# A hybrid decoder layer on one core: another task order and other priorities in the mixer, and a last post-norm by token block with a shorter root on VectorE

## The chip, the cores and the metric

One core of a Trainium2 chip runs the whole layer as one program. The metric is device time in microseconds (us), lower is better. The engines are TensorE (PE, with its weight loads shown apart as PEld), VectorE (DVE), ScalarE (ACT), GpSimd (POOL) and SyncE (SP), whose queue issues nearly all DMAs.

## The reference, cut to what matters

512 tokens, 1024 channels, fp32. One layer is a half-weighted SwiGLU feed-forward (FFN1), a token mixer with three branches, and a second half-weighted feed-forward (FFN2), each between two RMS norms.

```python
def rms_norm(x, gain):
    y = x * lax.rsqrt(jnp.mean(x * x, axis=-1, keepdims=True) + 1e-6)
    return y * gain
...
h = swiglu(rms_norm(x, ffn1_pre_norm), ffn1_w_gate, ffn1_w_up, ffn1_w_down)   # hidden width 2816
x = x + 0.5 * rms_norm(h, ffn1_post_norm)
u = rms_norm(x, mix_pre_norm)
# columns of u @ w_in feed: A native sparse attention (8 heads of 64), B gated DeltaNet (4 heads of 128,
# chunked, with a triangular solve), C cross-attention into 256 memory tokens (4 heads of 128)
merged = sum_b sigmoid(u @ w_branch_gate)[b] * (o_b @ w_branch_b)
x = x + rms_norm(merged @ w_out, mix_post_norm)
h = swiglu(rms_norm(x, ffn2_pre_norm), ffn2_w_gate, ffn2_w_up, ffn2_w_down)
x = x + 0.5 * rms_norm(h, ffn2_post_norm)          # the last post-norm, and the output
```

## The kernel before

Every large product is made of three fp32r matmuls (L117 to L119): each weight tile of 128x512 is loaded (`wraw`, DMA at L105), rounded on ScalarE (`whi`, L106), and the rest is taken by a subtraction (`wlo`, L109) on VectorE, or on GpSimd for every n-th load of a task when `pool_every` is n (0: never). A product of one output tile over 1024 channels is 24 matmuls of 128x512.

The layer runs in five parts: FFN1, its down projection (tasks of `order0`), the DeltaNet part of the mixer with the projections (`order`), attention and branch merge (`order2`), `w_out` with the mixer's post-norm (`order3`), then FFN2 with its own down projection and the last post-norm.

The order of the work is written out by hand in the table `PRM`. `tasks` calls one small function for each name of a list; the letter is the function, the digits its arguments. The framework gives every instruction a priority by its place in the program, `off` lifts a task by that many places, and at build time a planner with its own cost estimates fills one fixed queue for each engine from the instructions that it thinks ready, the first by priority ahead. On the chip each engine works through its queue in order and waits at the head. So a list entry does not fix a place, it moves a task's instructions in five queues, and a late input at the head holds back everything behind it on that engine.

Names of tasks that matter below. In `order`: `c` h s is a convolved projection for head h (24 matmuls, then VectorE and ScalarE), `h` h s its norm and transposes, `r`, `l`, `k` the decay rows and the small matrices of a head, `b` i the forward substitution for a pair of heads (30 dependent small VectorE operations, L719 and L721, with DMA round trips through DRAM, L712, L723, L726), `e` i its expansion (`Dm`, `DT`, L739), `d` i k a level of block inversion (L757 to L774, alternating PE and VectorE), `s` i n a chunk of the recurrence, `o` i the output norm (`dory`, `on`, L823, transposes `pot`), `z` a projection of 96 matmuls, `q` i a query projection, `x` w the input of the compression (16 VectorE additions `X`, L900), `f` and `p` the compression itself. In `order0`: `d` i a down projection half, `p` and `n` post-norm and norm, `t` the transposes, `k` h and `v` keys and values of the memory tokens (`mkv`, `pmv`). In `order2`: `K` the key stacks, `S`, `P`, `V`, `W` attention, `C` the compressed branch, `G`, `A`, `U` the cross-attention, `M` br j one merge tile. In `order3`: `s` the splits of the merged rows, `d` i h the product with `w_out` for token half i and column half h, `p`, `n`, `t` as above, `g` the load of the gain.

The last post-norm handles token blocks 0 and 1 together behind the first half of the FFN2 down projection, then block 2, then block 3, through `postnorm(last=True)` (L219): for each column half a square with a running sum on ScalarE (`junk`, L211), a product with the gain on VectorE (`pre`, L237), the sum of the two halves (`ssp`, L245), the root by 9 VectorE operations (`rsqrt`, L129 to L139), and the scaled addition to the residual. Blocks 0, 1 and 3 make that addition on VectorE (L260); block 2 (`spread=True`) scales on ScalarE (L257) and adds on GpSimd (L258). Each half is stored from SP's queue (L262). The last eight weight tiles of block 3 run behind those of block 2 on PE, so that block 2's post-norm has matmuls beside it and block 3's has none.

Of the kernel before, what the change touches and what calls it, by code (L numbers as in the profile page):

```python
# [10 lines left out]
F32 = mybir.dt.float32  # L11
F32R = mybir.dt.float32r
BF16 = mybir.dt.bfloat16
I32 = mybir.dt.int32
# [3 lines left out]
P = 128  # L18
# [15 lines left out]
PAD = 88  # L34


PRM = {'order': ['i', 'a', 'w', 'c01', 'h01', 'c00', 'c10', 'c02', 'r0', 'h00', 'h02', 'c12', 'k0', 'h10', 'c22', 'l0', 'c11', 'h11', 'h12', 'r1', 'z', 'k1', 'c21', 'l1', 'h22', 'b0', 'c20', 'h21', 'e0', 'r2', 'h20', 'c32', 'l2', 'c31', 'd00', 'h31', 'k2', 'r3', 'c30', 'd01', 'l3', 'b1', 'd02', 'x0', 's00', 'e1', 'd10', 'h32', 'x1', 'd11', 'h30', 's01', 's02', 's03', 'q0', 'p0', 'o0', 'k3', 'p1', 'q3', 'p2', 'p3', 'd12', 's10', 'p4', 'q1', 'p5', 's11', 'p6', 'p7', 's12', 'q2', 'f', 's13', 'o1'], 'dma': {'l': 'sync', 'b': 'sync', 'd': 'scalar', 'c': 'sync', 'r': 'sync'}, 'off': {'b0': 300, 'h31': 400, 'h00': 20, 'r1': 50, 'h32': 50, 'h11': 200, 'h12': 200, 'd10': 100, 'A01': 100, 'A10': 100, 'A11': 100, 'A20': 100, 'A31': 100, 'A21': 200, 'x0': 20, 'x1': 20, 'C2': 50, 'L': 200, 'S310': 400, 'S001': 20, 'S311': 400, 'A30': 100, 'r0': 400, 'd02': 20, 's11': 50, 'V20': 400, 'l3': 100, 'q1': 20, 'f': 400, 'l1': 20, 'h20': 100, 'h22': 100, 'r3': 50, 'P010': 100, 'y': 100, 'h02': 50, 'S101': 20, 'A00': 100, 'Q0': 50, 'Q1': 50, 'Q2': 50, 'Q3': 50, 'P110': 400, 'V31': 50, 'd01': 200, 'o0': 400, 'p0': 50, 'p1': 50, 'p2': 50, 'p4': 50, 'p5': 50, 'p6': 50, 'p7': 50, 'b1': 20, 'h01': 100, 'M15': 20, 'P201': 400, 'e0': 100, 'e1': 100, 'o1': 20, 'q0': 50, 'q2': 20, 'h21': 20, 'd11': 50, 'p3': 50}, 'ph': 'e', 'po': 'ss', 'xpd': (0, 1, 2), 'order2': ['K1', 'K0', 'B', 'M10', 'C3', 'Q0', 'C0', 'Q1', 'S000', 'S001', 'P001', 'C1', 'P000', 'S010', 'C2', 'S011', 'V00', 'P010', 'S100', 'P011', 'S110', 'Q2', 'V01', 'P100', 'S101', 'W0', 'P101', 'S111', 'Q3', 'M12', 'V10', 'P110', 'S200', 'P111', 'S210', 'V11', 'P200', 'M14', 'S201', 'M15', 'P201', 'S211', 'W1', 'V20', 'P210', 'M11', 'P211', 'V21', 'S301', 'S300', 'W2', 'P301', 'S311', 'P300', 'L', 'M13', 'S310', 'G0', 'V30', 'P310', 'G2', 'M16', 'P311', 'V31', 'W3', 'A00', 'M00', 'M17', 'A01', 'G1', 'U0', 'A10', 'M05', 'A11', 'G3', 'A30', 'A31', 'U1', 'U3', 'M03', 'A20', 'A21', 'U2', 'M07', 'M22', 'M02', 'M20', 'M24', 'M06', 'M27', 'M21', 'M01', 'M26', 'M23', 'M04', 'M25'], 'order0': ['d0', 'p0', 'n0', 't0', 'd1', 'k2', 'k0', 'p2', 'p3', 'k1', 'n1', 'v', 'k3', 't1'], 'order3': ['s2', 's3', 's7', 's6', 's1', 's5', 's0', 's4', 'd01', 'd00', 'g', 'p0', 'd10', 'n0', 't0', 'd11', 'p1', 'n1'], 't3': (('mm', 'r'), ('e', 's')), 'pool': {'W2': 2, 's13': 3, 'k0': 0, 'k1': 0, 'k2': 0, 'k3': 2, 'p3': 1, 'C0': 0, 'C1': 0, 'C2': 0, 'C3': 2, 'S310': 0, 'L': 3, 'd11': 3, 'p0': 1, 'p1': 1, 'p2': 1, 'p4': 2, 'p5': 1, 'p6': 1, 'p7': 1, 'S311': 0, 'h01': 0, 'h00': 0, 'h02': 0, 'h10': 0, 'h11': 0, 'h12': 0, 'h22': 0, 'h21': 0, 'h20': 0, 'h31': 0, 'h30': 3, 'h32': 0, 'i': 2, 'P011': 2, 'c21': 0, 'd01': 2, 'S000': 0, 'S001': 0, 'S010': 0, 'S011': 0, 'S100': 0, 'S101': 0, 'S110': 0, 'S111': 0, 'S200': 0, 'S201': 0, 'S210': 0, 'S211': 0, 'S300': 0, 'S301': 0, 'M24': 2, 'G2': 2, 'A01': 0, 'M10': 2, 'M15': 2, 'M12': 2, 'M14': 2, 'M13': 2, 'M17': 2, 'M11': 2, 'M16': 2, 'M23': 0, 'M27': 3, 'M01': 2, 'M00': 2, 'M03': 0, 'M07': 2, 'M06': 0, 'M22': 2, 'M04': 2, 'M20': 2, 'M26': 3, 'M02': 0, 'M21': 2, 'M25': 2, 'M05': 2, 'c11': 1, 'o1': 3, 'P000': 2, 'P001': 1, 'P010': 2, 'P100': 2, 'P101': 2, 'P110': 2, 'P111': 2, 'P200': 2, 'P201': 2, 'P210': 2, 'P211': 2, 'P301': 0, 'P300': 2, 'P310': 2, 'P311': 2, 'c12': 0, 'b1': 1, 'x0': 0, 'x1': 0, 'V21': 0, 'c30': 0, 'c01': 0, 'c02': 0, 'c00': 0, 'c10': 0, 'c22': 0, 'c20': 0, 'c31': 0, 'c32': 0, 's01': 3, 'A31': 0, 'd12': 0, 'y': 2, 'G0': 2, 'G1': 2, 'G3': 2, 'U3': 0, 'W3': 2, 'r1': 2, 's12': 3, 'U2': 0, 'Q0': 2, 'Q1': 2, 'Q2': 2, 'Q3': 1, 's00': 3, 's02': 2, 's03': 3, 's10': 3, 's11': 3, 'e1': 2, 'd00': 1, 'U0': 0, 'U1': 0, 'l2': 0}, 'pool3': {'d00': 3, 'd01': 3, 'd10': 3, 'd11': 3, 'p1': 2, 't1': 3, 't0': 3, 's5': 2, 's7': 2, 's1': 2, 's0': 2, 's3': 2, 's6': 2, 's2': 2, 's4': 2, 'q0': 1}, 'pool0': {}, 'off0': {'p3': 20, 'n1': 50, 't1': 100}, 'off3': {'s1': 20, 's5': 200, 'g': 200, 't0': 400}, 'tt': ('e', 's'), 'order_s': ['t00', 'w10', 'w00', 'y', 't01', 't02', 'w01', 't03', 'w11', 'R0', 'F000', 'x', 'F101', 'n', 'F200', 't10', 't11', 't12', 't13', 'c', 'F110', 'B', 'F211', 'F011'], 't0': ('e', 's'), 'rs': ((0, 0), (0, 0)), 'ra': (1, 1), 'warm': 8, 'pools': {'F000': 0, 'F101': 0, 'F200': 0, 'F011': 0, 'F110': 0, 'F211': 0, 'w10': 0, 'w11': 0, 't00': 0, 't01': 0, 't02': 0, 't03': 0, 't13': 0, 't10': 0, 't11': 0, 't12': 0, 'w00': 0, 'w01': 0}, 'ptc': 'vvs', 'cva': 'v', 'offs': {'t13': 100, 'R1': 400}, 'vnc': 's', 'sp3': 0, 'hsc': 'vv', 'sf2': 2, 'psc': 'vvvv', 'sp1': 0, 'vbs': 'v', 't1c': 'vs', 'sgv': 256}


class Body:  # L40
# [84 lines left out]
    def rsqrt(self, ss, n, scale, eps, name):  # L125
# [13 lines left out]
        v.scalar_tensor_tensor(y, z, 1.5 * c, y, op0=OP.add, op1=OP.mult)  # L139
        return y  # L140

    def norm(self, xs, tbs, spread=False, junk=()):

        nc = self.nc
        n = len(tbs)
        ss = self.sp.tile([P, n], F32, tag=f"ss{n}", name="ss")
        for i, b in enumerate(tbs):
            jk = junk[i] if junk else self.tp.tile([P, D], BF16, tag="tmpa", bufs=2, name="junk")
            if spread:
                nc.vector.tensor_tensor_reduce(jk, xs[b], xs[b], 1.0, 0.0, op0=OP.mult, op1=OP.add, accum_out=ss[:, i : i + 1])  # L150
            else:
                nc.scalar.activation(jk, xs[b], AF.Square, accum_out=ss[:, i : i + 1])
        r = self.rsqrt(ss, n, 1.0 / D, EPS, "rn")
        for i, b in enumerate(tbs):
            nc.vector.tensor_scalar(xs[b][:, :512], xs[b][:, :512], r[:, i : i + 1], None, op0=OP.mult)
            nc.scalar.activation(xs[b][:, 512:], xs[b][:, 512:], AF.Copy, scale=r[:, i : i + 1])
# [62 lines left out]
            self.nc.vector.tensor_scalar(gb, gb, float(f), None, op0=OP.mult)  # L219
        return gb  # L220

    def postnorm(self, acc, x, gb, sc, tbs, store, tmp, pre=None, s2=None, last=False, spread=False, early=False):

        nc = self.nc
        n = len(tbs)
# [10 lines left out]
                    t = pre[h, i] = tmp()  # L236
                    nc.vector.tensor_tensor(t, acc[h][i], gb[:, h], op=OP.mult)  # L237

        if last or early:
            gain(0)  # L240
        self.sumsq(acc[1], s2, 1, n)
        if early:
            gain(1)
        ss = self.sp.tile([P, n], F32, tag="ssp", name="ssp")
        nc.vector.tensor_tensor(ss, s2[:, 0], s2[:, 1], op=OP.add)  # L245
        if last:
            gain(1)
        r = self.rsqrt(ss, n, sc * sc / D, EPS, "rp")
        if sc != 1.0:
            nc.vector.tensor_scalar(r, r, float(sc), None, op0=OP.mult)  # L250
# [2 lines left out]
        for i, b in enumerate(tbs):  # L253
            for h in range(2):
                c = slice(h * 512, h * 512 + 512)
                if spread:
                    nc.scalar.activation(pre[h, i], pre[h, i], AF.Copy, scale=r[:, i : i + 1])  # L257
                    nc.gpsimd.tensor_tensor(x[b][:, c], x[b][:, c], pre[h, i], op=OP.add)  # L258
                else:
                    nc.vector.scalar_tensor_tensor(x[b][:, c], pre[h, i], r[:, i : i + 1], x[b][:, c], op0=OP.mult, op1=OP.add)  # L260
                if last:
                    nc.sync.dma_start(store[b * P : (b + 1) * P, c], x[b][:, c])  # L262
            if not last:
                nc.sync.dma_start(store[b * P : (b + 1) * P], x[b])

    def ffn_tile(self, n, f, t, xh, xl, RB, H, banks=None, tags=("mm", "mm"), pre=None):

# [836 lines left out]
    def run(self):  # L1104
# [241 lines left out]
        with tc.tile_pool(name="f2", bufs=1) as fp, contextlib.ExitStack() as x1:  # L1346
# [33 lines left out]
            for tbs, acc in parts:  # L1380
                for h in range(2):
                    t0 = tbs[0] * P
                    step = (lambda k: self.hsplit(H, Hh, Hl, k, slice(t0, t0 + 256))) if h == 0 else None
                    self.down_half(Hh, Hl, "ffn2_d", FT, tbs, acc[h], h, lor if h and t0 else (), step, t0)
            self.post_gain("ffn2_post", 0.5, gb)
            pre = self.cp.tile([P, 4, 512], F32, tag="mth", name="pre")
            pre = iter([pre[:, i % 4] for i in range(8)])
            tmp = lambda: next(pre)
            (tbs, acc), (_, c) = parts
            self.postnorm(acc, x, gb, 1.0, tbs, self.out, tmp, last=True)  # L1390
            for i in range(2):
                self.postnorm([c[0][i : i + 1], c[1][i : i + 1]], x, gb, 1.0, (2 + i,), self.out, tmp, last=True, spread=i == 0)


def host_layout(i):
# [98 lines left out]
```

## Time and profile before

| what | value |
|---|---|
| median of three runs | 1378.45 us (1367.98, 1378.45, 1382.18) |
| the profiled execution | 1365.18 us, span 1363.4 us |
| TensorE busy | 1332.1 us, 98% of the span |
| VectorE, ScalarE, GpSimd busy | 897.0, 719.1, 146.1 us |
| mean granted clock of TensorE | 0.996 |

The span runs from the first to the last instruction. A matmul is shown busy for longer than the step to the next one, so a busy PE says that work is in flight, not that it runs at its peak.

### The profile page before, as it was taken

To read this page: it belongs to the slowest core of one execution; us is meant where nothing else is said; L and a number is where in the kernel's file an instruction comes from. 1 tells how busy PE (TensorE), PEld (TensorE's weight loads), DVE (VectorE), ACT (ScalarE), POOL (GpSimd) and SP (SyncE) were. 2 spreads that over 40 slices of the span, in tenths; PEclk is the share of its full clock that TensorE was granted. 3 is DMA by queue.
4 is the path that set the end of the run, shared out by engine and by line. 5 is a ranking of instruction groups with operands and counts; after the bars stand their busy time and mean duration, and the time that the engine had idled before them with its cause. 6 is when DMAs were issued, how large, how long until landed. Compare 5 with 4: busy or idle time off the path is not lost.

```text
span 1363.4 us, 21808 instructions
## 1 busy us (share of the span) xinstructions
PE 1332.1 (98%) x7839; PEld 1130.3 (83%) x7839; DVE 897.0 (66%) x1797; ACT 719.1 (53%) x1542; POOL 146.1 (11%) x132
## 2 busy tenths in 40 slices
PE   9999999999999999999999999999999999999997
PEld 8889999787887878677777777888788899998886
DVE  6897875777558576646876424223587778766765
ACT  7556664766555553216654334323585565646643
POOL 0020000000011312003110121333300000000000
PEclk9999999999999999999999999999999999999999
DMA  7643331676654332423121222532744433317673
GB/s 254 194 147 109 109 110 32 209 244 209 190 176 125 98 100 63 113 82 118 46 63 47 70 63 92 164 100 93 243 136 148 134 121 98 121 33 261 194 224 101
DMA packets 107453, 178.32 MB, mean 131 GB/s; under 512 B 18908, under 2 KB 28496, under 8 KB 107344
## 3 DMA queue, kind: packets, MB, share of 16 engines
q1 hardware_dynamic: 107056, 176.67, 41.8%
q8 instruction: 61, 1.00, 0.3%
q14 instruction: 48, 0.39, 0.1%
q10 hardware_dynamic: 288, 0.26, 0.1%
HBM read 166.84 MB, written 10.01 MB: 130 GB/s over the span
## 4 chain that ended last, share of the span: by engine, by line
PE 49%; DVE 3%; ACT 1%; issue 1%; DVEq 0%; ACTq 0%
PE pfm L119 5%; PE pfm L117 5%; PE pfm L118 5%; PE smm L406 5%; PE se L406 3%; PE po L1051 2%; PE ss L406 2%; PE ps L1019 2%; PE ppt L1039 1%; PE acc_mm L117 1%; PE acc_mm L118 1%; PE acc_mm L119 1%; PE acc_e L118 1%; PE acc_e L117 1%; PE acc_e L119 1%; PE acc_s L117 1%
## 5 line engine op out<-in xcount | busy, mean ns | idle before, releaser
L106 ACT CAST whi<-wraw 128x512 fp32r<-128x512 f32 (+1 forms) x314 | 189.8, 616 | 185.3 <-PE pfm L119 70.3
L109 DVE TENSOR_TENSOR wlo<-wraw,whi 128x512 fp32r<-128x512 f32 (+1 forms) x270 | 184.1, 690 | 143.6 <-ACT whi L106 139.6
L118 PE MATMUL pfm<-xth,wlo 128*128 128x512 f32 x384 | 154.9, 405 | 2.6 <-DVE wlo L109 2.6
L117 PE MATMUL pfm<-xth,whi 128*128 128x512 f32 x384 | 155.7, 406 | 1.1 <-DVE drz L134 0.7
L119 PE MATMUL pfm<-xtl,whi 128*128 128x512 f32 x384 | 154.0, 402 | 0.0
L118 PEld LDWEIGHTS pfm<-xth,wlo 128*128 128x128 f32 x384 | 72.3, 189 | 19.3 <-DVE wlo L109 3.2
L117 PEld LDWEIGHTS pfm<-xth,whi 128*128 128x128 f32 x384 | 72.4, 189 | 18.5 <-issue 3.9
L119 PEld LDWEIGHTS pfm<-xtl,whi 128*128 128x128 f32 x384 | 72.4, 189 | 15.4 <-issue 1.0
L109 POOL TENSOR_TENSOR wlo<-wraw,whi 128x512 fp32r<-128x512 f32 (+1 forms) x41 | 51.1, 1246 | 243.0 <-ACT whi L106 196.4
L106 ACT CAST ringh<-ringr 128x512 fp32r<-128x512 f32 x82 | 50.1, 620 | 42.4 <-DMA ringr<-in_ffn_d_dram 11.2
L406 PE MATMUL smm<-thi,fset 128*128 128x256 f32 x384 | 69.5, 279 | 0.0
L109 DVE TENSOR_TENSOR wlo<-ringr,ringh 128x512 fp32r<-128x512 f32 x75 | 51.4, 689 | 21.8 <-PE acc_e L119 8.7
L406 PEld LDWEIGHTS smm<-thi,fset 128*128 128x128 f32 x384 | 58.5, 188 | 0.2
L422 DVE TENSOR_TENSOR up<-smm,s 128x256 f32<-128x256 f32 x32 | 13.6, 424 | 67.2 <-ACT se L419 67.2
L406 PE MATMUL smm<-thi,fxtl 128*128 128x256 f32 x192 | 53.6, 279 | 0.6 <-DVE fxtl L388 0.6
L406 PE MATMUL smm<-thi,fxth 128*128 128x256 f32 x192 | 53.3, 278 | 0.0
L406 PE MATMUL se<-thi,fset 128*128 128x256 f32 x256 | 46.7, 280 | 0.0
L1022 ACT ACTIVATE Pm<-Pm,nm 128x128 f32<-128x128 f32 (+1 forms) x64 | 35.6, 557 | 11.9 <-DVE nm L1021 11.6
L258 POOL TENSOR_TENSOR xb<-xb,pre 128x512 f32<-128x512 f32 x2 | 2.5, 1277 | 356.7 <-ACT pre L257 356.7
L123 DVE TENSOR_TENSOR Hl<-H,Hh 128x256 fp32r<-128x256 f32 x88 | 35.0, 420 | 7.0 <-ACT Hh L122 5.5
L406 PEld LDWEIGHTS se<-thi,fset 128*128 128x128 f32 x256 | 39.1, 187 | 0.0
L379 DVE TENSOR_TENSOR fs<-fq 128x1024 f32<-128x1024 f32 x32 | 38.9, 1217 | 0.0
(550 smaller groups left out, 3979.3 us busy)
## 6 DMA issues: line engine op xcount, KB each, us to landing
wraw<-in_ffn_d_dram SPq DMA_DIRECT2D x94, 256.0 KB, 2.9
ringr<-in_ffn_d_dram SPq DMA_DIRECT2D x82, 256.0 KB, 2.9
fq<-in_ffn_g_dram SPq DMA_DIRECT2D x64, 256.0 KB, 2.9
fq<-in_ffn_u_dram SPq DMA_DIRECT2D x64, 256.0 KB, 2.7
wraw<-in_w_gate_dram SPq DMA_DIRECT2D x48, 256.0 KB, 2.8
wraw<-in_ffn_u_dram SPq DMA_DIRECT2D x34, 256.0 KB, 3.2
wraw<-in_ffn_g_dram SPq DMA_DIRECT2D x34, 256.0 KB, 3.5
woraw<-in_w_out_dram SPq DMA_DIRECT2D x32, 256.0 KB, 2.9
```

Source lines behind the costliest of these rows:

```text
L106: nc.scalar.copy(hi, raw)
L109: eng.tensor_tensor(lo, raw, hi.bitcast(F32), op=OP.subtract)
L117: t.matmul(out, lh, rh, start=first, stop=False)
L118: t.matmul(out, ll, rh, start=False, stop=False)
L119: t.matmul(out, lh, rl, start=False, stop=last)
L123: return self.nc.vector.tensor_tensor(lo, src, hi.bitcast(F32), op=OP.subtract)
L379: add = lambda *x: v.tensor_tensor(*x, op=OP.add)
L406: m = lambda x, y, **kw: te.matmul(out, x, y, skip_group_check=True, **kw)
L1019: te.matmul(s[:, : max(n, 256)], A[:, qb * P : qb * P + P], K[j][:, : max(n, 256)], start=j == 0, stop=j == 1)
L1022: nc.scalar.activation(pm, pm, AF.Exp, bias=nm[:, qb : qb + 1], scale=-1.0, accum_out=sm[:, qb : qb + 1])
L1039: te.transpose(pt[:, o : o + P], Pm[:, self.OFF[qb] + kb * P : self.OFF[qb] + kb * P + P], self.ident)
L1051: te.matmul(po[64 * g : 64 * g + 64, kb * P :], vt[:, kb, br * P + 64 * g : br * P + 64 * g + 64], pts[g][:, col[kb] : col[kb] + n], start ...
```

## The change

1. `order`, `order0`, `order2`, `order3` list the same tasks in another order, and some priorities (`off`, `off0`, `off3`, `offs`) and shares of GpSimd (`pool`, `pool3`) differ.
2. The last post-norm runs through a new function `ending`, one token block at a time, always on VectorE. The gain carries the constant `RK`, the root is `rsqrt1`: 7 operations, of which the first adds the two halves' sums of squares.

```diff
-'order': i a w c01 h01 c00 c10 c02 r0 h00 h02 c12 k0 h10 c22 l0 c11 h11 h12 r1 z k1 c21 l1 h22 b0 c20 h21 e0 r2 h20 c32 l2 c31 d00 h31 k2 r3 c30 d01 l3 b1 d02 x0 s00 e1 d10 h32 x1 d11 h30 s01 s02 s03 q0 p0 o0 k3 p1 q3 p2 p3 d12 s10 p4 q1 p5 s11 p6 p7 s12 q2 f s13 o1
+'order': i a w c01 h01 r0 c00 c10 c02 l0 h00 h02 c12 k0 h10 c22 c11 h12 h11 h22 r1 k1 l1 b0 c21 z h21 e0 c20 r2 h20 c32 l2 c31 d00 h31 k2 r3 d01 l3 b1 d02 x0 s00 e1 d10 c30 h32 x1 d11 h30 s01 s02 s03 q0 q3 p0 o0 p1 p2 p3 k3 d12 s10 p4 q1 p5 s11 p6 p7 s12 s13 o1 q2 f
-'order0': d0 p0 n0 t0 d1 k2 k0 p2 p3 k1 n1 v k3 t1
+'order0': d0 p0 n0 t0 d1 k2 k0 p2 p3 v k3 n1 k1 t1
-'order2': K1 K0 B M10 C3 Q0 C0 Q1 S000 S001 P001 C1 P000 S010 C2 ... P110 S200 P111 S210 V11 P200 ... W3 A00 M00 M17 A01 G1 U0 A10 M05 A11 G3 A30 A31 U1 U3 M03 A20 A21 U2 M07 M22 M02 M20 M24 M06 M27 M21 M01 M26 M23 M04 M25
+'order2': K1 K0 B M10 Q0 C0 Q1 S000 C3 S001 P001 P000 C1 S010 C2 ... P110 M12 S200 P111 V11 P200 S210 ... M17 V31 W3 A00 M00 A01 G1 U0 M05 A10 A11 G3 A30 U1 A31 U3 M03 M06 A20 A21 U2 M07 M22 M20 M02 M24 M27 M21 M23 M01 M04 M26 M25
-'order3': s2 s3 s7 s6 s1 s5 s0 s4 d01 d00 g p0 d10 n0 t0 d11 p1 n1
+'order3': s3 s7 s2 s6 s1 s5 s0 s4 d00 d01 d11 g p0 n0 t0 d10 p1 n1
 # priorities, old -> new (0: none)
 off:  b1 20->200  s00 0->200  s13 0->50  s11 50->100  c20 0->50  c11 0->20  k2 0->20  h00 20->0  p5 50->20  Q1 50->200  C2 50->0  P011 0->400  P010 100->50  M14 0->200  M03 0->20  A20 100->400  A21 200->20  U0 0->100
 off0: d0 0->200  k1 0->400  k2 0->400  t1 100->0
 off3: d10 0->200  p0 0->200
 offs: w10 0->200  t03 0->20
 # every n-th subtraction on GpSimd, old -> new (0: none); entries of tasks that load weights
 pool: K1 2->3  M10 2->1  M06 0->1  G3 2->0
 pool3: d11 3->0
```

```diff
+    RK = -0.5 * 0.375**3
+    def rsqrt1(self, s0, s1, scale, eps):
+        v = self.nc.vector
+        m, y, z = (self.sp.tile([P, 1], F32, tag=f"r1{s}", name=f"r1{s}") for s in "myz")
+        v.tensor_scalar(m, s1, float(scale), s0, op0=OP.mult, op1=OP.add)
+        v.tensor_scalar(y.bitcast(I32), m.bitcast(I32), -0.5, 1597463007.0, op0=OP.mult, op1=OP.add)
+        v.scalar_tensor_tensor(z, y, m, y, op0=OP.mult, op1=OP.mult)
+        v.scalar_tensor_tensor(z, z, -10.0 / 3, z, op0=OP.add, op1=OP.mult)
+        v.scalar_tensor_tensor(y, z, 5.0, y, op0=OP.add, op1=OP.mult)
+        v.scalar_tensor_tensor(z, y, m, y, op0=OP.mult, op1=OP.mult)
+        v.scalar_tensor_tensor(y, z, -3.0 / 0.375**2, y, op0=OP.add, op1=OP.mult)
+        return y
+    def ending(self, acc, x, gb, b, store, tmp):
+        nc = self.nc
+        s = self.sp.tile([P, 2], F32, tag="s21", name="s21")
+        pre = [tmp(), tmp()]
+        for h in range(2):
+            jk = self.tp.tile([P, 512], BF16, tag="tmpa", bufs=2, name="junk")
+            nc.scalar.activation(jk, acc[h], AF.Square, accum_out=s[:, h : h + 1])
+            nc.vector.tensor_tensor(pre[h], acc[h], gb[:, h], op=OP.mult)
+            if not h:
+                nc.vector.tensor_scalar(s[:, :1], s[:, :1], 1.0 / D, EPS, op0=OP.mult, op1=OP.add)
+        r = self.rsqrt1(s[:, :1], s[:, 1:], 1.0 / D, EPS)
+        for h in range(2):
+            c = slice(h * 512, h * 512 + 512)
+            nc.vector.scalar_tensor_tensor(x[b][:, c], pre[h], r, x[b][:, c], op0=OP.mult, op1=OP.add)
+            nc.sync.dma_start(store[b * P : (b + 1) * P, c], x[b][:, c])
...
-            self.post_gain("ffn2_post", 0.5, gb)
+            self.post_gain("ffn2_post", 0.5 * self.RK, gb)
...
-            (tbs, acc), (_, c) = parts
-            self.postnorm(acc, x, gb, 1.0, tbs, self.out, tmp, last=True)
-            for i in range(2):
-                self.postnorm([c[0][i : i + 1], c[1][i : i + 1]], x, gb, 1.0, (2 + i,), self.out, tmp, last=True, spread=i == 0)
+            for tbs, acc in parts:
+                for i, b in enumerate(tbs):
+                    self.ending([acc[0][i], acc[1][i]], x, gb, b, self.out, tmp)
```

`postnorm` loses its branches `last` and `spread`; what is left of it is what the other two post-norms ran before.

## Rows read from the trace of the kernel before

**Rows 1.** Windows by stage: length, busy PE, PEld, DVE, ACT, POOL, granted clock, DMA.

```profile
393.00:636.00 243.00, 233.80 (x1337) 188.65 (x1336) 149.42 (x404) 104.18 (x250) 43.02 (x49) 0.99 0.35 99
636.00:954.60 318.60, 316.91 (x1505) 242.10 (x1504) 157.46 (x418) 137.35 (x328) 73.48 (x55) 1.00 0.28 86
...
1233.40:1355.20 121.80, 121.34 (x531) 98.91 (x529) 83.94 (x162) 70.67 (x146) 1.10 (x1) 1.00 0.67 202
1355.20:1363.40 8.20, 0.00 (x0) 0.00 (x0) 3.99 (x13) 0.69 (x2) 1.42 (x2) 0.81 0.34 129
sum 1363.40, PE 1332.12 PEld 1130.30 DVE 897.04 ACT 719.09 POOL 146.13; mean PE 166.52 PEld 141.29 DVE 112.13 ACT 89.89 POOL 18.27
```

**Rows 2.** The same view, 50 us of merge tiles (128x512 matmuls alone).

```profile
850.00:900.00 50.00, 50.00 (x217) 40.55 (x216) 14.76 (x23) 16.07 (x28) 15.71 (x11) 1.00 0.48 151
```

**Rows 3.** Timeline of the end: start, duration, engine, line, operation, idle and its releaser.

```profile
1354.10 2.51 POOL L258 TENSOR_TENSOR xb<-xb,pre 128x512 f32<-128x512 f32 x2 [356.74 <-ACT pre L257]
...
1355.75 0.19 ACT L211 ACTIVATION_READ_ACCUMULATOR junk<-acc_s 128x1 f32 x1
1355.98 0.65 DVE L245 TENSOR_TENSOR ssp<-s 128x1 f32<-128x1 f32 x1 [2.71 <-ACT junk L211]
1356.56 0.68 DVE L237 TENSOR_TENSOR pre<-acc_s,gb 128x512 f32<-128x512 f32 x1
1357.16 0.14 DVE L129 TENSOR_SCALAR rpm<-ssp 128x1 f32<-128x1 f32 x1
...
1358.68 0.16 DVE L139 SCALAR_TENSOR_TENSOR rpy<-rpz,rpy 128x1 f32<-128x1 f32 x1
1358.87 1.42 DVE L260 SCALAR_TENSOR_TENSOR xb<-pre,rpy,xb 128x512 f32<-128x512 f32 x2
```

**Rows 4.** Timeline, the same operations for block 2.

```profile
1325.02 0.69 DVE L237 TENSOR_TENSOR pre<-acc_e,gb 128x512 f32<-128x512 f32 x1 [0.71 <-ACT junk L211]
...
1350.43 0.16 DVE L245 TENSOR_TENSOR ssp<-s 128x1 f32<-128x1 f32 x1 [5.05 <-ACT junk L211]
```

**Rows 5.** Waits of PE from 393 to 636 us: total, times, longest.

```profile
PE pfm L118 <- DVE wlo L109: 2.6, 1, 2.6
PE pt L761 <- DVE Dm L739: 1.7, 1, 1.7
PE ptk L655 <- DVE kn L648: 1.7, 1, 1.7
PE pot L824 <- DVE on L823: 1.2, 1, 1.2
```

**Rows 6.** Timeline of DVE around the expansion of the first pair.

```profile
519.90 2.15 DVE L739 TENSOR_TENSOR Dm<-Dc,msk 128x512 f32<-128x512 f32 x2 [1.98 <-DMA Dc<-dD]
```

**Rows 7.** Timeline of DVE before the longest wait.

```profile
544.49 2.68 DVE L900 TENSOR_TENSOR X<-pfm,pos 64x248 f32<-64x248 f32 x7 [0.95 <-PE pfm L119]
...
553.12 0.68 DVE L109 TENSOR_TENSOR wlo<-wraw,whi 128x512 fp32r<-128x512 f32 x1
```

**Rows 8.** Windows just behind the longest wait.

```profile
554.00:556.00 2.00, 2.00 (x8) 1.18 (x8) 1.93 (x8) 0.00 (x0) 0.00 (x0) 0.70 0.47 131
556.00:558.00 2.00, 2.00 (x6) 0.48 (x4) 1.73 (x9) 0.00 (x0) 0.00 (x0) 0.50 0.04 8
```

**Rows 9.** Waits of PE from 242 to 393 us.

```profile
PE pmv L117 <- ACT mkv L517: 1.4, 1, 1.4
```

**Rows 10.** Waits of PE from 954.6 to 1030 us.

```profile
PE ptr L166 <- DVE xa L155: 1.3, 1, 1.3
PE acc_s L117 <- ACT whi L106: 1.0, 1, 1.0
```

**Rows 11.** Timeline of ACT before the wait of `acc_s`.

```profile
987.06 1.06 ACT L152 ACTIVATE junk<-xa 128x1024 bf16<-128x1024 f32 x1 [2.91 <-DVE xa L260]
```

**Rows 12.** The page's costliest groups: GpSimd's subtractions.

```profile
L109 POOL TENSOR_TENSOR wlo<-wraw,whi 128x512 fp32r<-128x512 f32 (+1 forms) x41 | 51.1, 1246 | 243.0 <-ACT whi L106 196.4
```

**Rows 13.** Timeline of the first matmul's wait.

```profile
7.53 0.39 PE L117 MATMUL pg<-xth,whi 128*128 128x256 f32 x1 [1.57 <-ACT whi L106]
```

## The prediction before the run

> **What bounds the kernel now.** I read the busy shares of the page first, then the windows by stage, then PE's waits stage by stage, then the timeline around each wait. The reader is to see that PE is busy for 1332.1 of 1363.4 us [rows 1]: all idle time of PE together is 31.3 us, and no order of tasks can give more than that, beside what PE loses at a lower clock. The idle time is not spread evenly. The DeltaNet stage (393 to 636 us) has 243.0 - 233.8 = 9.2 us of it, attention and merge only 318.6 - 316.9 = 1.7 us, FFN2's down projection 0.5 us, and the end, where PE has nothing left, 8.2 us [rows 1]. So the long `order2` list, which the change rewrites most, works on a stage with next to nothing to win; `order` and the end are where the time can move.
>
> **The end.** It is one chain on VectorE. ScalarE's last sum of squares is there at 1355.75 + 0.19 = 1355.94, and the scaled addition begins at 1358.87: 2.93 us [rows 3]. In them stand the sum of the halves (0.62 until the next start), the gain product (0.60, from 1356.56 to 1357.16) and nine root operations (1.71, or 0.19 each). The sum of the halves takes 0.65 us, where the same operation took 0.16 for block 2 [rows 3, 4]; it ends at 1356.63, and GpSimd's additions for block 2 end at 1354.10 + 2.51 = 1356.61 [rows 3]. I read that as VectorE held up by GpSimd.
> After the change the chain is the gain product, if it still stands behind the square, and seven operations: 0.04 + 0.60 + 7 x 0.19 = 1.97 us. That removes 2.93 - 1.97 = 0.96 us: the held-up sum, which the first root operation takes in, and two root operations. The two additions (1.42 for both) and the stores stay. Would the gain product run beside the square, 0.60 more would go, 1.56 in all. I take 0.96, since in the rows the product of block 2 is idle until the square of the same accumulator has ended, though nothing of the square goes into it [rows 4]; the new code also writes the square first.
> The Trainium skill gives a reason why the two are kept apart: "PSUM — Partial Sum Buffer", section "PSUM bank collisions raise a hardware error", has it that two engines must not be on one bank and the same partitions at once, readers included. By that rule the gain of the end is the 0.96, without it the 1.56; the row agrees with the rule.
> What moves onto VectorE is block 2's addition, two operations of 0.7 us, in a stretch in which VectorE stood idle for 2.71 us before the last sum [rows 3]. I cost it at nothing; if that cover were gone it would be 1.4 us. The first two blocks now take two short roots for one longer one, 6 small operations or 1.1 us more, beside matmuls in a stage where PE idles 0.5 of 121.8 us and VectorE is busy for 83.9 [rows 1]: nothing, with 1.1 us as the bound. The stores keep their places on SP's queue behind the last weight loads; block 2's leave earlier.
>
> **The DeltaNet order.** Four waits make 7.2 of the stage's 9.2 us [rows 5].
> - `Dm`, 1.7 us: the expansion `e0` waits for the round trip of `b0` through DRAM (VectorE was idle for 1.98 us until `Dc` landed) [rows 6]. The new list puts `z`, 96 matmuls, between `b0` and `e0`; at 50.0/217 = 0.23 us each [rows 2] that is 22 us of work for PE while the trip runs. I expect this wait gone.
> - `wlo`, 2.6 us, the longest: a subtraction stands in VectorE's queue behind the 16 additions `X` (7 of them 2.68 us), a root and half of `b1`'s substitution, from 544.49 to 553.12 [rows 7]. Behind it PE runs at a granted clock of 0.70 and then 0.50, the lower of its two levels, for 4 us [rows 8]: 0.3 x 2 + 0.5 x 2 = 1.6 us of full-speed work lost on top. The new list moves the projection `c30` (24 matmuls, 5.5 us) to just before `h32 x1`, and lifts `b1`, so that its chain runs ahead of the additions. Both work on this wait; neither removes the additions. If gone, 4.2 us.
> - `on`, 1.2 us: the output norm `o1` was the last task, now `q2` (24 matmuls) and `f` are behind it. I expect it covered.
> - `kn`, 1.7 us, `h01` at the stage's start: `r0` moves to just behind it, which adds work to the same queues; I count nothing.
>
> **The other lists.** `order0`: `pmv` waits 1.4 us for ScalarE to clear a bank of the key product [rows 9]; `v` now stands ahead of `n1` and `k1`, `k1` and `k2` are lifted; 1.4 us if gone. Behind `v` on ScalarE's queue are then the squares of `n1`, and `t1` and the first task of `order` wait for those: the bound on the bad side is the same 1.4. `order3`: `acc_s` waits 1.0 us for a rounded weight, because ScalarE's queue has the norm's square at its head (idle 2.91 us until the residual is there) [rows 10, 11]. `d10` is now lifted by 200, so its roundings go ahead of such squares, and `d11` comes earlier; 1.0 us if gone. The 1.3 us of `ptr` [rows 10] belong to the chain of post-norm and norm itself, which keeps the same two products as cover; I count nothing. `order2`: its stage has 1.7 us of idle time in all; nothing, within 1.7 either way. `w10` lifted: PE's first wait on a rounded weight is 1.57 us [rows 13]; the weight comes earlier, the activations later by one transfer; nothing, within 0.6 either way, which is about one rounding.
> Shares of GpSimd: `M06` takes 3 subtractions and `M10` one or two more, `G3` and `d11` give up three or four, so there is at most one more, of 1.25 us [rows 12], in a stage in which PE waits for almost nothing. I count nothing; the bound is the 1.25. Against this part speaks the Trainium skill, "SBUF — State Buffer", section "Who interferes with whom": an operation of VectorE with two inputs from SBUF and one of GpSimd that reads SBUF block each other fully. The trace agrees with it at the one place costed above (0.65 for 0.16); by that rule the moved subtractions would hold up VectorE by up to their own 1.25 us each, and it gives no other sum as long as PE has its weights ahead.
>
> **The sum.** The waits with a reason to go are 1.7 + 4.2 + 1.2 + 1.4 + 1.0 = 9.5 us. But the planner filled the old queues by its own estimates and did not see these waits, or it would have filled them; the new queues come out of the same estimates and will have waits of the same kind elsewhere. I take half, 4.75, as the net, and 0.96 at the end: 1365.18 - 5.7 = 1359.5 us against the profiled execution. The three runs shown lie 2.8, 13.3 and 17.0 above that execution, 11.0 in the mean, by something that the profile does not show; so I forecast 1359.5 + 11 = 1370.5, say 1370, against the median of 1378.45. A measurement of this kernel, with runs 1% apart, can tell about 1% from no change; 1% is 13.8 us.
>
> **The rivals.**
> 1. All the named waits go and none comes: 0.96 + 9.5, so 1354.7, or 1365.7 for runs. For it: each of them has a task moved into it or a priority that bears on it. Against: the waits [rows 5] come from fixed queues, and 27 priorities changed at once. Chance 0.2.
> 2. The waits only move, and the end alone gains: 1364.2, or 1375. For it: the stage's idle time is of one kind, a VectorE that is late, and VectorE's work is the same. Chance 0.2.
> 3. Slower: `c30` is missing where it was. In the old list it stands between `r3` and `d01`, and its 24 matmuls are PE's only wide work beside the inversion levels `d01` and `d02`, which alternate PE and VectorE. If it covered them fully, 5.5 us become idle time, and a wait of that length brings the clock down as the 2.6 us did, 1.6 more. With the waits otherwise as in 2: 1365.18 - 0.96 + 7.1 = 1371.3, or 1382 for runs. It decides if PE's waits on `T`, `px` and `DT` behind `d01` add up to more than the 4.2 us of `wlo`. Against it: `l3`, `k2` and `r3` leave other work near. Chance 0.15, of which a third is beyond 1% slower.
>
> **How the numbers follow.** The forecast has 0.45. The range goes from rival 1 with the fastest of the run offsets, 1354.7 + 2.8 = 1357, to rival 3 with the median offset, 1371.3 + 13.3 = 1384; the costs bounded above (1.4, 1.7, 1.25, 0.6) lie inside. Faster by over 1% is below 1364.7: half of rival 1, a quarter of the forecast, a tenth of rival 2, 0.23 in all. Slower by over 1% is above 1392: 0.05. Within 1%: 0.72.
>
> **What would show it.** At the end: no separate sum of the halves, no GpSimd at all behind 1350 us, and about 2.0 us from the last square's end to the first addition. In PE's waits between 393 and 636 us: `pt` from `Dm` and `pot` from `on` missing, `wlo` shorter, and the granted clock without its dip, so that PE's idle time there falls from 9.2 to some 5 us. In `order3` no wait of `acc_e` or `acc_s` on `whi`. The prediction is wrong if the stage's idle time stays at 9 us or grows behind `d01`, if idle time appears in attention and merge, or if the runs scatter about another offset than those of before.

## The result and the profile after

| | before | after |
|---|---|---|
| median of ten runs | 1378.12 us (1365.75 to 1382.18) | 1360.55 us (1358.28 to 1363.56) |
| the profiled execution | 1365.18 us, span 1363.4 us | 1360.60 us, span 1358.8 us |
| TensorE, VectorE, ScalarE, GpSimd busy | 1332.1, 897.0, 719.1, 146.1 us | 1330.2, 899.9, 717.7, 142.3 us |

The ratio of the means is 0.9898 [0.9865, 0.9931]: 1% faster. The medians lie further apart, 17.6 us or 1.3%, because the runs of before are of two kinds. The prediction said 1370 us (1357 to 1384), with 1359.5 for a profiled execution and 11 us on top for the runs. The profiled execution came out at 1360.6; the 11 us did not come at all.

One thing must be known for every comparison below: the runs of the kernel before lie in two groups, whatever chip they ran on. Of the ten beside the result four are at 1365.75 to 1367.98 and six at 1377.80 to 1382.18. In the later comparisons, where each run's mean granted clock is listed, the lower group has .995 to .998 and the upper .983 to .988. The kernel after has one group, at .994 to .999. So the 17.6 us between the medians are 5.9 us between the lower groups (1366.46 to 1360.55) and 11.7 us that the upper group adds to the median of before. Both executions profiled here are of the lower kind, so their traces can explain the first part only.

Stage by stage, by the start of the first matmul of each stage in the two traces:

| stage | before, us | after, us | difference |
|---|---|---|---|
| up to the first matmul | 7.53 | 9.49 | +1.96 |
| FFN1 | 235.34 | 235.04 | -0.30 |
| `order0` | 153.75 | 152.65 | -1.10 |
| `order` (DeltaNet) | 239.23 | 236.92 | -2.31 |
| `order2` (attention, merge) | 318.81 | 319.11 | +0.30 |
| `order3`, FFN2's wide products | 279.40 | 276.87 | -2.53 |
| FFN2's down projection | 121.10 | 121.08 | -0.02 |
| last matmul to the end | 8.21 | 7.64 | -0.57 |

These are two single executions, and other traces tell which differences repeat. `order0` took 153.3 and 153.9 us in two further traces with the old lists (`e1`, `e2` below) and 151.6 and 152.0 in two with the new ones (`e3`, `e4`); `order3` with FFN2's wide products took 279.3 and 279.2 against 277.3 and 277.4. But `order` took 237.8 and 236.8 with the old list and 237.8 and 237.7 with the new one. The executions with the old list spread over 2.4 us (239.2 for before, and these two), so the 2.31 us of the table are within the scatter: between executions of the lower kind no gain of the DeltaNet stage is shown.

The windows by stage after (columns as in [rows 1]):

```profile
394.00:634.00 240.00, 231.89 (x1347) 189.25 (x1346) 154.66 (x410) 105.25 (x254) 45.31 (x50) 1.00 0.34 99
634.00:953.20 319.20, 318.08 (x1506) 241.05 (x1505) 155.67 (x416) 137.12 (x326) 75.00 (x56) 1.00 0.28 86
...
1351.20:1358.80 7.60, 0.00 (x0) 0.00 (x0) 3.30 (x10) 0.69 (x2) 0.00 (x0) 0.63 0.30 112
sum 1358.80, PE 1330.19 PEld 1128.07 DVE 899.94 ACT 717.72 POOL 142.27; mean PE 166.27 PEld 141.01 DVE 112.49 ACT 89.71 POOL 17.78
```

PE is idle for 240.00 - 231.89 = 8.1 us of the DeltaNet stage, where it was 9.2 [rows 1]. PE's waits there, after, against [rows 5]:

```profile
PE pfm L117 <- DVE cacc L635: 3.0, 1, 3.0
PE ptk L678 <- DVE kn L671: 2.1, 2, 1.7
PE pkk L722 <- POOL kbT L700: 1.3, 2, 0.8
PE ptm L117 <- ACT whi L106: 0.8, 1, 0.8
PE pot L847 <- DVE on L846: 0.4, 1, 0.4
```

`Dm` and `wlo` are gone, `on` is down from 1.2 to 0.4, and the granted clock stays at 1.00 where it dipped to 0.50 [rows 8]. The wait of `pmv` [rows 9] and that of `acc_s` on `whi` [rows 10] are gone too. New is `cacc`, 3.0 us. What VectorE and GpSimd did just before it (timeline: start, duration, engine, operation):

```profile
498.82 1.36 POOL L707 TENSOR_TENSOR kd<-kn,dec 128x512 f32<-128x512 f32 x1 [2.38 <-DVE kn L671]
500.14 1.51 POOL L762 TENSOR_TENSOR DT<-Dc,msk 128x512 f32<-128x512 f32 x1
501.61 1.74 POOL L700 TENSOR_TENSOR kbT<-k,rowsb 128x512 f32<-128x512 f32 x1
```

```profile
499.19 3.01 DVE L762 TENSOR_TENSOR Dm<-Dc,msk 128x512 f32<-128x512 f32 x2
502.12 1.78 DVE L762 TENSOR_TENSOR DT<-Dc,msk 128x512 f32<-128x512 f32 x1
503.82 0.74 DVE L217 TENSOR_SCALAR cacc<-pfm,cw 128x512 f32<-128x512 f32 x1
```

The expansion `e0`, lifted by 100 places, stands in front of the additions `cacc` that PE needs, and its three operations take 4.8 us beside three of GpSimd; the two that write `Dm` take 3.01 us of it, where they took 2.15 before [rows 6].

The end, after, against [rows 3]:

```profile
1351.76 0.19 ACT L164 ACTIVATION_READ_ACCUMULATOR junk<-acc_s 128x1 f32 x1
1351.98 0.69 DVE L165 TENSOR_TENSOR pre<-acc_s,gb 128x512 f32<-128x512 f32 x1 [1.54 <-ACT junk L164]
1352.59 0.20 DVE L148 TENSOR_SCALAR r1m<-s 128x1 f32<-128x1 f32 x1
...
1353.02 0.22 DVE L150 SCALAR_TENSOR_TENSOR r1z<-r1y,r1m 128x1 f32<-128x1 f32 x1
1353.27 0.16 DVE L151 SCALAR_TENSOR_TENSOR r1z<-r1z 128x1 f32<-128x1 f32 x1
...
1354.11 1.42 DVE L171 SCALAR_TENSOR_TENSOR xb<-pre,r1y,xb 128x512 f32<-128x512 f32 x2
```

From the last square's end (1351.95) to the addition it is 2.16 us, where it was 2.93. The gain product still starts only when the square has ended, and GpSimd does nothing there.

### The profile page after: what moved, and what is told of

It is laid out like the page before. It is cut to its first block, busy times and chain, and to the rows that moved or that the text cites. A ratio compares the mean times of both kernels' runs of the same rounds, so it can differ in the third digit from the quotient of the medians.

```text
span 1358.8 us, 21802 instructions
## 1 busy us (share of the span) xinstructions
PE 1330.2 (98%) x7839; PEld 1128.1 (83%) x7839; DVE 899.9 (66%) x1802; ACT 717.7 (53%) x1538; POOL 142.3 (10%) x129
## 4 chain that ended last, share of the span: by engine, by line
PE 88%; DVE 5%; ACT 2%; DMA 2%; issue 1%; POOL 0%; SPq 0%; ACTq 0%; DVEq 0%; POOLq 0%
PE smm L429 10%; PE pfm L117 7%; PE pfm L118 7%; PE pfm L119 7%; PE se L429 7%; PE ss L429 3%; PE po L1074 2%; PE ps L1042 2%; PE acc_e L118 2%; PE acc_e L119 2%; PE acc_e L117 2%; PE sr L429 2%; PE acc_s L119 1%; PE acc_s L117 1%; PE acc_s L118 1%; PE so L429 1%
## 5 line engine op out<-in xcount | busy, mean ns | idle before, releaser
L1044 DVE CUSTOM_DVE_ANT_0 Pm<-ps,tbl 128x128 f32<-128x128 f32 (+1 forms) x64 | 29.7, 484 | 10.9 <-PE ps L1042 10.3
```

The costliest lines, as they stand in the source:

```text
L1044: v.tensor_tensor_reduce(pm, s[:, :n], tb[:, SEQ - n :], -1.0, 3e38, op0=OP.add, op1=OP.min, accum_out=nm[:, qb : qb + 1])
```

## The experiments

Each group of three or four ran on one chip beside the same runs of the kernel before. Where a kernel has two groups, its lower group is compared with the lower group of before.

**The kernel before again (`e1_before_again`)**, no edit.

> The kernel before, unchanged. Ten runs of it lie in two groups, 1366 to 1368 us (four) and 1378 to 1382 us (six), and none between; the changed kernel has one group, 1358 to 1364. Theory A: the upper group belongs to this kernel's queues, that is, to a race between two arrivals that one order settles early and the other late. Then these runs fall in the same two groups, near half and half, and a profile of an upper run shows some 13 us of PE idle time or of lower clock in one or a few places that the lower profile lacks. Theory B: the upper group is the chip's state at the time. Then the runs lie in one group, and the other kernels of this call scatter along with it.

Measured: two groups again, four runs at 1365.25 to 1368.41 and eight at 1377.69 to 1381.31; median 1377.97. Its trace has the first matmul at 9.19 us instead of 7.53 [rows 13]. So a first matmul at 9.49 us, as in the kernel after, is no sign of a cost of the change: the old kernel has both.

**The two halves of the change.** `e2_end_only`: the new `ending`, the old lists. `e3_order_only`: the new lists, the old ending.

> The kernel before with the new last post-norm alone; every task order and priority is the old one. Theory A (the end gains only what its chain lost): 0.6 to 1.0 us less than before in each group, so 1365.5 and 1378, and the two groups stay. Rival: the end, by using GpSimd no more, also settles the two groups; then one group near 1366 and a ratio near 0.992.

> The new orders and priorities with the old last post-norm. Theory A (the order makes nearly all of the gain, and its queues also end the two groups): 1361 to 1362 us in one group, ratio 0.990 to 0.991. Rival (the groups are the end's doing): two groups, 1361 and 1374.

Measured: `e2` keeps both groups; the lower is 1363.67 at the median, that of before 1364.46: -0.8 us. From the last matmul to the end it takes 7.94 us, against 8.42 in `e1`. `e3` has one group of nine runs, 1359.48 to 1363.56, median 1361.70: -2.8 us against the lower group, with a ratio of 0.9905 [0.9867, 0.9942]. The upper group belongs to the lists, not to the ending. The two gains make 3.6 us; the whole change has 5.9 in the runs of the result, and on this chip `e4`, which is the kernel after but for its start, has 4.4. Comparisons across chips are no finer than that.

**The start (`e4_old_start`)**, the kernel after with the old priorities of the first lists:

```diff
-'offs': {'t13': 100, 'R1': 400, 't03': 20, 'w10': 200}
+'offs': {'t13': 100, 'R1': 400}
```

> The changed kernel with the old priorities of the first stage (w10 and t03 back to none). The changed kernel issues the first weight ahead of the activations, its first product starts at 9.5 us in place of 7.5 and its first stage ends 1.6 us later. Theory A (the start is a loss that the rest carries on to the end): first product near 7.5 us and 1.5 to 2 us less than the changed kernel, 1358.5 to 1359. Rival (the start is covered by the first stage's own slack, or its clock is given back): no difference from 1360.5, or the two groups return, if the start is what settles them.

Measured: 1360.06 us, six runs from 1358.72 to 1362.92, first matmul at 8.43. The kernel after has 1360.55. The lift of `w10` shows neither cost nor gain in the time; theory A, that it costs 1.5 to 2 us, fell. Single traces start at 7.53 to 9.41 us without the lift and at 8.96 to 10.16 with it.

**What starts the long low clock, first idea (`e5_q0_pool`)**: the kernel before, with `'q0': 1` added to the shares of GpSimd in `pool`, so that the late subtraction of [rows 7] leaves VectorE's queue.

> The kernel before, with one edit: the two weight subtractions of task q0 go to GpSimd, which is idle there, so that the matmul that waits 2.6 us at 551 us no longer stands behind VectorE's additions. So far every run of the old order lies at 1363 to 1368 us with a mean granted clock of 0.995 to 0.998, or at 1376 to 1381 with 0.984 to 0.987: the upper group is some 27 us more at the lower clock. Theory A: what starts that long stretch is the 2.6 us wait, behind which the profile shows the clock fall. Then the wait is gone, the upper group with it, all runs lie at 1360 to 1364 us with a clock above 0.99, ratio near 0.990. Theory B: the stretch starts at another place, or at any place by chance. Then two groups as before, each lower by 2 to 4 us at most.

Measured: the `wlo` wait is gone, and both groups come down by 3 us, 1362.22 (before 1365.40) and 1375.51 (before 1379.11) at their medians; but there are still six runs in each. The longest wait of [rows 5] is worth 3.2 us, of the 4.2 that the prediction gave it, and it is not the origin of the upper group. That idea fell.

**`c30` and `b1` (`e6_c30_b1`, `e7_c30_b1_back`)**: the two edits that the prediction gave the `wlo` wait to, made alone in the old kernel, and undone alone in the new one.

```diff
-'order': ... k2 r3 c30 d01 l3 b1 d02 x0 s00 e1 d10 h32 x1 ...     'off': 'b1': 20
+'order': ... k2 r3 d01 l3 b1 d02 x0 s00 e1 d10 c30 h32 x1 ...     'off': 'b1': 200
```

> The kernel before, with the two edits of the change that bear on the 2.6 us wait: c30 stands before h32, and b1 is lifted by 200. Theory A (these two edits are what the change's main gain comes from): the wait of `wlo` is gone or below 1 us, one group of runs, 1361 to 1365 us. Theory B (the gain needs the whole list): the wait stays or comes back on another input behind `d01`, and two groups stay, 1365 and 1378.

> The changed kernel with those two edits undone: c30 before d01 and b1 at 20. Theory A: the `wlo` wait is back at 2 us or more behind `x1`, and a part of the runs goes up to 1373 to 1376 us with a clock below 0.99, the others stay at 1361 to 1363. Theory B: one group, within 3 us of the changed kernel's 1360.5.

Measured: `e6` has two groups, 1362.19 and 1374.69, so -3.2 us in the lower one; in its trace the `wlo` wait is gone. `e7` has one group at 1365.44, 4.9 us above the kernel after (5.9 if both are taken against the lower group on their own chip). Neither run met either of its theories: in `e6` the wait goes and the groups stay, and in `e7` the wait does not come back, no upper group comes, and the time is still longer. Rival 3 of the prediction (PE left without wide work behind `d01`) is refuted from both sides: with `c30` late nothing waits on `T`, `px` or `DT` for as much as a microsecond. The profiled execution of `e7`, the slowest of its runs, spends 7.2 us more in `order` than the kernel after. Its clock is at the lower level from 505.9 to 512.7 us (never in that stage of the kernel after), and PE, back from the `cacc` wait at 506.7, loses 3.0 us of work by it; a wait on `qs` makes 1.0. Its waits and its clock do not show the rest, and whether its other runs have the same I cannot say.

**GpSimd's share (`e8_no_gpsimd_sub`)**: the kernel after with every count in `pool` and `pool3` set to 0.

> The changed kernel with every weight subtraction of the mixer and of w_out on VectorE, none on GpSimd (pool and pool3 all zero). Theory A (a subtraction on GpSimd holds up VectorE for nearly its own 1.25 us wherever VectorE has two inputs from SBUF, so the share pays nothing): 1358 to 1361 us, GpSimd's busy time down by some 50 us, VectorE's up by less than 30. Theory B (VectorE has no room in the attention stage, and the share relieves it): waits of PE on `wlo` of 3 us or more in all, 1363 to 1368 us.

Measured: 1359.46 us, 1359.08 to 1361.55; GpSimd busy 83.6 us instead of 142.3, VectorE 928.6 instead of 899.9. The 58.7 us that GpSimd gives up become 28.7 us of VectorE, and no time is lost by it in all (5.9 us below the lower group, as the kernel after on its own chip). One wait went, `wlo` on GpSimd (1.0 us, in `order2`), and one came, `KL`, 1.5 us:

```profile
PE pfm L117 <- DVE cacc L635: 3.0, 1, 3.0
PE ptk L678 <- DVE kn L671: 2.1, 2, 1.7
PE pfm L117 <- DVE KL L1015: 1.5, 1, 1.5
```

**What starts the long low clock, second idea.** Left were the `Dm` wait and the tail of `order`. `e9_z_late` moves one name in the kernel before; `e10_tail` reorders only the tail of it; `e11_z_early` puts `z` back in the kernel after.

```diff
e9 -... h12 r1 z k1 c21 l1 h22 b0 c20 h21 e0 ...
e9 +... h12 r1 k1 c21 l1 h22 b0 c20 z h21 e0 ...
e10 -... q0 p0 o0 k3 p1 q3 p2 p3 d12 s10 p4 q1 p5 s11 p6 p7 s12 q2 f s13 o1
e10 +... q0 q3 p0 o0 p1 p2 p3 k3 d12 s10 p4 q1 p5 s11 p6 p7 s12 s13 o1 q2 f
e11 -... h22 r1 k1 l1 b0 c21 z h21 e0 ...
e11 +... h22 r1 z k1 l1 b0 c21 h21 e0 ...
```

> The kernel before, with one name of its list order moved: z (96 projection matmuls) from ahead of k1 to between b0 and h21, where the new list has it. Theory Z (the long half-clock stretch that makes the old order's upper group of runs begins where PE waits 1.2 to 1.7 us for Dm and then meets only the sparse inversion products): the Dm wait is gone, and all runs lie in one group at a granted clock of .993 or more, 1361 to 1366 us; median 12 below the kernel before's upper group. Theory T (it begins in the tail of order, behind q0): two groups stay, some 13 us apart, as in e5, and the lower one is 1 to 2 us below that of before.

> The kernel before, with the names of order from q0 on in the new list's sequence (q3 earlier, k3 later, s13 and o1 ahead of q2 and f), all else old. Theory T: one group, 1361 to 1367 us. Theory Z: two groups, the lower at 1362 to 1367 us with the on wait gone, the upper some 13 us above at a granted clock near .985.

> The kernel after, with z put back ahead of k1 and all else new. Theory Z: the Dm wait comes back (1 to 2 us near 520 us), and with it an upper group of runs near 1373 to 1376 us at a granted clock near .985; the lower group at 1361 to 1364. Theory T: one group at 1360 to 1364 us.

Measured: beside them the kernel before has ten runs around 1365.7, sixteen around 1378.3, and two between (1371.22 and 1374.41, at .992 and .991). `e9` has one group of twelve runs, 1364.90 to 1366.81. The single move of `z` takes the upper group away; it does not make the lower one any faster (+0.4 us). In its trace the `Dm` wait of 1.7 gives way to one on `zg` of 2.1, with the clock at its lower level for 3.4 us behind it; the `wlo` wait is missing too, and what takes its gain back I can't name. `e10` has both groups, 1360.98 and 1375.72 at their medians. So theory Z holds for the place, theory T falls. `e10`'s lower group is 4.7 us below that of before, more than the 1 to 2 expected. Its trace, which is of an upper run, does not say why: `on` is down from 1.2 to 0.3, and the `wlo` wait reads 0.3, but the same `wlo` still stands behind the same 16 additions in VectorE's queue. PE only meets these one matmul earlier, and the two waits make 2.2 us in place of 2.6:

```profile
565.87 0.47 PE L117 MATMUL pfm<-xth,whi 128*128 128x512 f32 x1 [1.83 <-DVE X L900]
566.68 0.79 PE L118 MATMUL pfm<-xth,wlo 128*128 128x512 f32 x1 [0.34 <-DVE wlo L109]
```

By luck the profiled execution of `e10` is one of the upper group (1375.72 us), so the long stretch can be seen. Up to `q0` its list is that of before. Windows around the `Dm` wait, first of `e10`, then of `e1`, a lower run of the kernel before (length, busy PE, granted clock, DMA share, GB/s):

```profile
516.00:520.00 4.00, 3.31 (x22) 1.00 0.56 98
520.00:524.00 4.00, 3.28 (x18) 0.75 0.05 19
524.00:528.00 4.00, 4.00 (x19) 0.50 0.23 66
...
544.00:548.00 4.00, 4.00 (x19) 0.50 0.02 4
548.00:552.00 4.00, 4.00 (x33) 0.83 0.23 66
```

```profile
516.00:520.00 4.00, 3.28 (x21) 1.00 0.56 107
520.00:524.00 4.00, 3.47 (x25) 1.00 0.02 6
524.00:528.00 4.00, 4.00 (x33) 1.00 0.22 66
```

The clock falls to its lower level at 522.0 and comes back at 549.3: 27.3 us at half clock, 13.7 us of work lost, which is nearly the distance between the groups (1375.72 - 1360.98 = 14.7). What PE did in it (line, operation, shapes, count, busy and mean ns of one):

```profile
L777 PE MATMUL pxt<-DT,T 128*128 128x64 f32 x32 | 7.4, 414 | 0.0
L768 PE MATMUL px<-T,DT 128*128 128x64 f32 x32 | 7.3, 410 | 0.0
L761 PE MATMUL pt<-Dm,LT 128*128 128x64 f32 x24 | 5.5, 419 | 0.1
L117 PE MATMUL pfm<-xth,whi 128*128 128x512 f32 x4 | 2.8, 701 | 0.0
```

Most of it, 20.2 us, are the small products of the block inversion behind `e0`; in `e1`, from 522 to 536 us, the same 88 products take 272, 270 and 275 ns. And just ahead of the fall stands the `Dm` wait, here 1.34 us:

```profile
518.92 0.39 PE L118 MATMUL pfm<-xth,wlo 128*128 128x512 f32 x1
520.65 1.11 PE L761 MATMUL pt<-Dm,LT 128*128 128x64 f32 x8 [1.34 <-DVE Dm L739]
```

In the profiled execution of before this wait is 1.7 us [rows 5], longer, and the clock stays at 1.00. So the wait alone does not bring the fall; something that differs from run to run decides. That the wait makes it possible is argued and not shown, since `e9` moves the wait and the work around it together. But the two go together in every kernel here: the six with a `Dm` wait of 1.0 us or more in their trace (before, `e1`, `e2`, `e5`, `e6`, `e10`) have an upper group, the eight without it have none. The Trainium skill, "TensorE: Matmul & The Clock Gate", section "What's actually happening", says that activity is judged on a beat that runs freely and does not start with the kernel; 59 of 105 runs of one list in the upper group agree with that, but no run here tested what decides.

`e11` missed the expectation of theory Z: one group at 1361.84 to 1365.41, median 1363.68, and no `Dm` wait. So in the new lists the upper group stays away with `z` in its old place too: moving `z` is enough in the old list, but the change holds something else that is enough as well. PE instead waits earlier and longer, for `Bt`, 5.1 us, and then meets the wide products of a projection:

```profile
501.23 0.77 PE L117 MATMUL pfm<-xth,whi 128*128 128x512 f32 x1 [5.13 <-DVE Bt L742]
501.80 0.63 PE L118 MATMUL pfm<-xth,wlo 128*128 128x512 f32 x1
```

In the profiled execution the clock falls there too, from 499.1 us on, and is back after 6.8 us, of which 2.1 still belong to the wait. So a long wait alone does not make an upper group: in these two traces a wait of 5.1 us ahead of wide products costs 2.3 us by the clock, one of 1.3 us ahead of the inversion's small products 13.7. The converse test, `z` early with the `Dm` wait in the new list, was not achieved.

**The new wait (`e12_e0_not_lifted`)**: the kernel after with `'e0': 100` changed to `'e0': 0` in `off`.

> The kernel after, with the task e0 without its lift of 100 places, so that VectorE takes the convolution's additions cacc between the expansion's operations Dm and DT rather than behind them. If the 3.0 us wait of pfm on cacc near 505 us comes from e0's operations in front of cacc, slowed by GpSimd's beside them, it shrinks below 1 us and the time falls by 2 to 3 us, to 1357 to 1359. If the wait only moves to Dm behind b0 or to another task, the time stays at 1360 to 1361.

Measured: 1357.91 us, six runs from 1357.24 to 1358.87, 7.8 us below the lower group of before on its chip, where the kernel after stood 5.9 below on its own. It is the fastest of all kernels here, some 2 us below the kernel after (2.6 by the medians, which are not of one chip). VectorE now takes the additions between `e0`'s operations, and the `cacc` wait is gone (timeline of VectorE, then GpSimd beside it):

```profile
498.11 1.54 DVE L762 TENSOR_TENSOR Dm<-Dc,msk 128x512 f32<-128x512 f32 x1
499.57 0.74 DVE L217 TENSOR_SCALAR cacc<-pfm,cw 128x512 f32<-128x512 f32 x1
500.23 1.12 DVE L762 TENSOR_TENSOR Dm<-Dc,msk 128x512 f32<-128x512 f32 x1
501.27 0.73 DVE L635 SCALAR_TENSOR_TENSOR cacc<-pfm,cw,cacc 128x509 f32<-128x509 f32 x1
501.93 0.88 DVE L762 TENSOR_TENSOR DT<-Dc,msk 128x512 f32<-128x512 f32 x1
...
499.07 1.73 POOL L700 TENSOR_TENSOR kbT<-k,rowsb 128x512 f32<-128x512 f32 x1
500.76 1.50 POOL L762 TENSOR_TENSOR DT<-Dc,msk 128x512 f32<-128x512 f32 x1
```

The longest wait that is new there is one on `cy`, 1.5 us. The additions, which read PSUM, take 0.73 to 0.74 us both beside GpSimd's operations and after them; `Dm` and `DT`, with both inputs in SBUF, go from 0.88 (here) to 1.78 us (in the kernel after). That agrees with the Trainium skill, "SBUF — State Buffer", section "Who interferes with whom": only operations that need the port pair shared with GpSimd block each other.

## Why the prediction was right, and where it was not

- **How far it was right.** The profiled execution, 1360.60, is near the 1359.5 forecast, and the lower groups are 5.9 us apart, where the sum had 5.7. The larger part of the measured 17.6, the 11.7 us of the upper group, was in no branch of the prediction. That 1360.55 still lies in the range is luck: the range's lower end came from rival 1 with the offset of the fastest run.
- **The step that failed** is in the sum: "so I forecast 1359.5 + 11". The 11 us were the mean distance of three runs of before from its profiled execution, carried over to a kernel with other lists. They were no offset of the runs but the share of an upper group, which the lists take away (`e3`); in the old list the place of `z` alone does it (`e9`), and the prediction itself named `z` as moved. One of its signs of being wrong, runs that scatter about another offset than before, is what came. Without the 11 us the forecast would have been 1359.5 against 1360.55. The text gave the warning sign, two runs 13.3 and 17.0 above and one 2.8, and took the mean of two kinds. The chances suffered with it: faster by over 1% had 0.23, and the ratio is 0.9898, just beyond.
- **Where the gain sits** was mis-sized too. Of the 9.5 us of waits 7.1 were in `order`, and PE's idle time there was to fall to some 5 us. It fell from 9.2 to 8.1, near the sign of being wrong ("stays at 9 us"), and the stage's length shows no gain beyond the scatter of single executions. What repeats in every trace is in `order0` (151 to 153 us with the new list, 153 to 154 with the old) and `order3`. So part of the good sum is luck.
- **The end**: predicted -0.96, from square to addition -0.77, at the end of the span -0.57 in the profiled pair and -0.48 from `e1` to `e2`. The mechanism was right (GpSimd off, two operations fewer, the product still behind the square). Mis-sized was "7 x 0.19" for the root: the three operations that take their scalar from a tile (`r1m` and the two products with it) last 0.20 to 0.22, the others 0.15 to 0.16, and from the first start to the addition it is 1.52 instead of 1.33. Of the 0.77 some 0.2 is not seen at the end of the span; where it goes between the stores was not tried.
- **`Dm`, 1.7**: gone, and by the step named (`e9`). It was mis-sized from below: as a wait worth nothing, since another took its place, as the place where the long low clock begins, worth the whole upper group.
- **`wlo`, 2.6 + 1.6**: gone; alone worth 3.2 us (`e5`, `e6`). The prediction gave it to `c30` and `b1`, which do it; but with both undone in the new lists it does not come back (`e7`), and with `z` moved alone it goes as well (`e9`), so these gains don't add up. Two readings were off: 8 of the 30 steps of `b1`'s substitution stand in front of the subtraction, not half, and 26 priorities changed, not 27.
- **`on`, `pmv`, `acc_s`, 1.2 + 1.4 + 1.0**: gone down to 0.4, 0 and 0. `order0` gained 1.1; `order3` and FFN2 gained 2.5, more than the 1.0 of the wait, in every kernel with the new `order3` (276.1 to 277.6 us in their traces, against 279.1 to 279.5 with the old). What the other 1.5 us are was not taken apart.
- **"I take half"**: 9.5 us of waits named, 4.75 taken. The stages of the lists gained 1.10 + 2.31 - 0.30 + 2.53 = 5.6 us in the profiled pair, of which the 2.31 are not shown to repeat; by the runs the lists alone gain 2.8 (`e3`). The reason given holds: waits of the same kind came elsewhere, `cacc` 3.0, `kbT` 1.3, `whi` 0.8, `wlo` 1.0.
- **What was costed at nothing** stayed so where it was looked at: `w10` (`e4`), GpSimd's shares, all of them at once (`e8`), `order2` (+0.3). Block 2's addition on VectorE was not tried alone; FFN2's down projection, in which it runs, stays at 121.1 us.
- **The rivals**: 1 (nothing comes in place) and 2 (waits only move) were both refuted, the first by the `cacc` wait in the trace, the second by `e3`, where the lists gain without the new ending; 3 by `e6` and `e7`.

## What to carry to other kernels

When the runs of one kernel lie in two groups, don't average them into an offset: look for a place where a short wait of PE is followed by many small matmuls, and try wide work in front of it. Count a wait's price by what PE does next, not by its length alone; and when a wait is gone from a list of waits, look whether the same chain holds PE up under another name. Before a stage of one trace is called faster, compare it with the same stage in a second execution of the same kernel. And when a task is lifted to end one wait, look at what it now stands in front of on its own engine's queue, and whether GpSimd works beside it: undoing one lift here gained more than the whole new ending.

## What the runs showed of the hardware that I had not expected

- With PE busy for 4.00 of every 4.00 us, the clock stayed at its lower level from 524 to 548 us; being busy in the profile's sense did not bring it back.
- The same instruction list was in the upper group in 59 of 105 runs of the kernel before, in the lower in 44 and between them in 2.
- Behind a wait of 3.0 us in the kernel after the clock stayed at 1.00, behind one of 1.34 us in `e10` it fell; `e3` and `e4`, with the same `order` as after, show 3.4 us of half clock at that same 3.0 us wait.
- A 128x1 operation of VectorE whose scalar comes from a tile takes 0.22 instead of 0.16 us, and up to 0.25 instead of 0.20 to the next start.
